# Gram products by pair of heads and ahead of the values, rests at every third column, put-off steps, and quarters of x

## The chip, the cores and the metric

One core of a Trainium2 chip runs the whole layer as one program. Its engines work side by side: TensorE (PE, matrix products), VectorE (DVE), ScalarE (ACT), GpSimd (POOL) and SyncE (SP, which here issues transfers). The metric is device microseconds for one execution. All times below are microseconds.

## The reference

A block of one layer over 256 tokens of width 2048, in float32. The normed input `h` goes through one wide projection, three branches work on the pieces, and their gated results go through a last projection:

```python
h = rms_norm(x, norm_g)
proj = h @ w_in
y_a = merge_heads(moba_attention(...)) * silu(z_a)          # 12 heads of 128
y_b = rwkv7_time_mix(r_b, k_b, v_b, lw, la, ...) * silu(z_b)  # 24 heads of 64
y_c = memory_cross_attention(q_c, mem_n, w_mem_kv) * silu(z_c)
merged = g_a * (y_a @ w_proj_a) + g_b * (y_b @ w_proj_b) + g_c * (y_c @ w_proj_c)
return rms_norm(x + merged @ w_out, final_norm_g)
```

The second branch is a recurrence over the tokens, for each head with a state of 64 x 64:

```python
sa = einsum('bhvk,bhk->bhv', state, a_t)
state = state * w_t + sa * b_t + v_t * k_t      # outer products
y_t = einsum('bhvk,bhk->bhv', state, r_t)
```

## The kernel before

**Main work.** All projections are jobs (class `Job`) that run one after the other in chunks of weights. A chunk of 128 KC x 256 weights is fetched (`raw`, three buffers), split into a high half by ScalarE (L270, a copy to fp32r) and a low half (L273, the rest, by VectorE or in the head by POOL) in `wt` (four buffers), and multiplied. A job in mode "fm" makes the result with features on partitions: for each of four k tiles and two halves of the features one product of 512 columns (L308: the high half with high and low of the input) and one of 256 (L309: the low half). That is eight pairs a chunk. A "wide" job has tokens on partitions and makes twelve products of 512 columns with each half chunk (L306). `prefetch` issues fetches and splits as far ahead as the buffers let it. The input side of the products is hT, the normed and transposed x, split in the same way.

**Side work.** Everything else is written as Python generators, lanes, which are stepped once behind every chunk (`step_lanes`); each yields after how many chunks it wants its next step, and can wait for flags that other lanes set. So the program order on every engine is fixed when the program is written out: a chunk of main products, then a step of each lane that is due, then the next chunk. `force` and `drain` step lanes with no main products between them, until a flag is set or no lane is left. Main products have four banks of PSUM (`pm`), side work has four (`psd`, `ps_side`), which are taken in turn.

**The second branch** runs for six groups of four heads. For a group, `pairs_lane` makes the decays and the tiles AR and BK, transposes two tiles for sums per head (L590) and then the values V and BK (L599 to L601, two sets, one bank each), once the values' job is done, and starts `rw_lane`. That lane computes Gram products of BK and AR (L622, 64 rows of the array each, two chunks of 128 tokens, for each two pairs of heads with two banks each), evacuated on VectorE (L626, L627). It sends 32 x 32 blocks through DRAM into NB and inverts them by a recursion over 31 columns on VectorE (L674, L678), with a rest for one chunk at every fourth column. X goes through DRAM again (XN), and a chain follows on TensorE: L700, L721, L743, L751 to L765 and the transposes of the result (L780), whose bank VectorE reads for the mean and the difference (L790). After a norm (L805 multiplies the values by a sum, L810 adds) comes a last transpose (L817). `attn_a` does the first branch for two heads a group: scores (L838, L840), a softmax (L851 to L861), transposes (L868) and the values' products (L876, L878), whose bank is kept until the gate zsa is there.

**The head.** `x_stats` sums squares of x and keeps TensorE at work with dummy transposes of the identity (L905). Then each quarter of x, 512 columns, is scaled (ScalarE L916 for one half of the tokens, VectorE L917 for the other), transposed (`turned`, L154, eight operations of 128 x 128 a quarter) and evacuated into hT: high halves on ScalarE (L159), low halves on VectorE (L162). `lora_pre` is called ahead of each of the first job's four chunks: it does quarters 0 and 1 ahead of chunk 0, and quarter c + 1 ahead of chunks 1 and 2.

## Time and profile before

| | us |
|---|---|
| three runs | 1478.37, 1479.20 (median), 1479.53 |
| the profiled execution | 1478.29 |
| its span | 1476.5 |
| TensorE busy | 1449.2 (98% of the span) |
| VectorE busy | 946.2 (64%) |
| ScalarE busy | 747.3 (51%) |
| GpSimd busy | 181.8 (12%) |

The span is the time from the first to the last instruction that the profiler records; the execution's own time is measured around it and is 1.8 longer. The busy share of TensorE includes products that are stretched or wait inside a group, so it hides small stalls; the lists of waits and the timelines show them one by one. The granted clock is 0.997 of full speed as a mean over the span.

### The profile page before, as it was taken

To read this page: it belongs to the slowest core of one execution; us is meant where nothing else is said; L and a number is where in the kernel's file an instruction comes from. 1 tells how busy PE (TensorE), PEld (TensorE's weight loads), DVE (VectorE), ACT (ScalarE), POOL (GpSimd) and SP (SyncE) were. 2 spreads that over 40 slices of the span, in tenths; PEclk is the share of its full clock that TensorE was granted. 3 is DMA by queue.
4 is the path that set the end of the run, shared out by engine and by line. 5 is a ranking of instruction groups with operands and counts; after the bars stand their busy time and mean duration, and the time that the engine had idled before them with its cause. 6 is when DMAs were issued, how large, how long until landed. Compare 5 with 4: busy or idle time off the path is not lost.

```text
span 1476.5 us, 22151 instructions
## 1 busy us (share of the span) xinstructions
PE 1449.2 (98%) x8315; PEld 1222.3 (83%) x8315; DVE 946.2 (64%) x1855; ACT 747.3 (51%) x1122; POOL 181.8 (12%) x252
## 2 busy tenths in 40 slices
PE   7999999999999999999999999999999999999997
PEld 6887888888888788788888888888888888888887
DVE  5778697796795786784666555655545545545555
ACT  5546546466456456445666454643443444444443
POOL 4312202212212222211100000000000000000011
PEclk9999999999999999999999999999999999999999
DMA  5665555456465465465575555566556556555753
GB/s 180 192 179 163 159 147 169 143 167 173 133 184 151 134 172 159 135 178 158 162 221 187 172 169 174 167 196 192 187 188 195 188 187 194 188 188 192 262 200 130
DMA packets 207968, 258.88 MB, mean 175 GB/s; under 512 B 28172, under 2 KB 146596, under 8 KB 207220
## 3 DMA queue, kind: packets, MB, share of 16 engines
q1 hardware_dynamic: 201872, 247.11, 54.5%
q10 hardware_dynamic: 4164, 6.71, 1.3%
q0 software_dynamic: 1824, 3.65, 0.8%
q8 instruction: 65, 1.06, 0.3%
q14 instruction: 43, 0.35, 0.1%
HBM read 253.74 MB, written 6.05 MB: 176 GB/s over the span
## 4 chain that ended last, share of the span: by engine, by line
PE 89%; DVE 4%; DMA 2%; ACT 1%; issue 1%; POOL 1%; SPq 0%; ACTq 0%; DVEq 0%
PE pm L306 43%; PE pm L308 24%; PE pm L309 12%; PE psd L622 2%; DVE wt L273 1%; DMA raw<-in_w_in_dram 1%; DVE fs_t L674 1%; PE psd L641 1%; PE psd L1037 1%; PE psd L743 1%; DMA NB<-d 1%; PE psd L154 1%; DMA x_sb<-in_x_dram 1%; ACT wt L270 1%; DVE X L678 1%
## 5 line engine op out<-in xcount | busy, mean ns | idle before, releaser
L273 DVE TENSOR_TENSOR wt<-raw,wt 128x1024 fp32r<-128x1024 f32 (+1 forms) x451 | 559.1, 1242 | 437.4 <-ACT wt L270 433.8
L270 ACT ACTIVATE wt<-raw 128x1024 fp32r<-128x1024 f32 (+1 forms) x452 | 477.2, 1057 | 494.0 <-PE pm L306 256.5
L308 PE MATMUL pm<-hT,wt 128*128 128x512 f32 (+1 forms) x1632 | 587.1, 402 | 0.0
L309 PE MATMUL pm<-hT,wt 128*128 128x256 f32 (+1 forms) x1632 | 458.5, 281 | 3.5 <-DVE wt L273 3.4
L308 PEld LDWEIGHTS pm<-hT,wt 128*128 128x128 f32 (+1 forms) x1632 | 305.7, 187 | 76.3 <-issue 4.2
L306 PE MATMUL pm<-wt,hT 128*128 128x512 f32 x1440 | 335.4, 391 | 0.0
L306 PEld LDWEIGHTS pm<-wt,hT 128*128 128x128 f32 x1440 | 268.6, 188 | 57.6 <-issue 1.7
L309 PEld LDWEIGHTS pm<-hT,wt 128*128 128x128 f32 (+1 forms) x1632 | 307.5, 188 | 6.2 <-DVE wt L273 6.0
L306 PE MATMUL pm<-wt,mg 128*128 128x512 f32 (+1 forms) x384 | 79.3, 367 | 0.0
L306 PEld LDWEIGHTS pm<-wt,mg 128*128 128x128 f32 x384 | 65.7, 189 | 12.5
L1183 POOL MEMSET sso<- 128x16 f32 x1 | 0.1, 117 | 607.0 <-PE pm L306 607.0
L674 DVE TENSOR_TENSOR fs_t<-X,NB 128x30 f32<-128x30 f32 (+13 forms) x354 | 64.9, 223 | 7.5 <-DMA NB<-d 7.1
L306 PE MATMUL pm<-wt,yas 128*128 128x512 f32 x288 | 67.6, 395 | 0.0
L306 PE MATMUL pm<-wt,ybs 128*128 128x512 f32 x288 | 67.6, 395 | 0.0
L323 POOL TENSOR_TENSOR lraw<-lraw,et 128x256 f32<-128x256 f32 (+1 forms) x38 | 45.1, 1207 | 167.2 <-ACT lraw L322 167.2
L306 PEld LDWEIGHTS pm<-wt,ybs 128*128 128x128 f32 x288 | 54.3, 188 | 12.6
L306 PEld LDWEIGHTS pm<-wt,yas 128*128 128x128 f32 x288 | 54.3, 188 | 12.7
L317 ACT ACTIVATE et<-pm 128x256 f32<-128x256 f32 (+1 forms) x112 | 42.6, 382 | 40.3 <-PE pm L309 37.6
L678 DVE TENSOR_TENSOR X<-X,fs_t 128x30 f32<-128x30 f32 (+13 forms) x354 | 56.3, 194 | 0.6
L306 PE MATMUL pm<-wt,mT 128*128 128x512 f32 x192 | 45.8, 395 | 0.0
L308 PE MATMUL pm<-mT,wt 128*128 128x512 f32 x128 | 45.4, 395 | 0.0
L306 PE MATMUL pm<-wt,ycs 128*128 128x512 f32 x192 | 45.3, 395 | 0.0
(299 smaller groups left out, 1324.3 us busy)
## 6 DMA issues: line engine op xcount, KB each, us to landing
raw<-in_w_in_dram SPq DMA_DIRECT2D x320, 512.0 KB, 3.7
raw<-in_w_mem_kv_dram SPq DMA_DIRECT2D x32, 512.0 KB, 3.5
raw<-in_w_out_dram SPq DMA_DIRECT2D x32, 512.0 KB, 4.4
raw<-in_w_proj_a_dram SPq DMA_DIRECT2D x24, 512.0 KB, 4.2
raw<-in_w_proj_b_dram SPq DMA_DIRECT2D x24, 512.0 KB
raw<-in_w_proj_c_dram SPq DMA_DIRECT2D x16, 512.0 KB, 4.4
NB<-d SPq DMA_DIRECT2D x24, 128.0 KB, 3.4
fr<-fd ACTq DMA_DIRECT2D x6, 385.0 KB
```

Of the source, the lines that this page charges most:

```text
L154: pe.transpose(pv[:, a, t], src[:, t, (k + a) * 128:(k + a + 1) * 128], ident)
L270: act.activation(w[:, :, 0], r, AF.Copy)
L273: eng.tensor_tensor(w[:, :, 1], r, w[:, :, 0].bitcast(FT), OP.subtract)
L306: pe.matmul(ps[:, 0:j.n], l, r, start=first and n == 0, stop=last and n == 2)
L308: pe.matmul(ps[0:j.m], hi, both, start=first, stop=last, skip_group_check=True)
L309: pe.matmul(ps[0:j.m, 256:512], lo, top, start=False, stop=last, skip_group_check=True)
L317: act.activation(t, ps[0:j.m, 256:512], AF.Copy)
L323: pool.tensor_tensor(j.dst[f], j.dst[f], t, OP.add)
L622: pe.matmul(pv[h][:, w].rearrange("p x t -> p (x t)"), BK[rows, q, c, w * 128:(w + 1) * 128], AR[rows, q, c].rearrange("p x t -> p (x t)") ...
L641: pe.matmul(pv[:, 2 * q + h], GS[:, c * 4 + 2 * q + h, 2], tok[:, q, c, rows], start=(c == 0), stop=True, skip_group_check=True)
L674: dve.tensor_tensor(t, X[:, k0:8, c:c + 1].to_broadcast([128, m, hi - lo]), NB[:, lo:hi, c].rearrange("p (o n) -> p o n", o=1).to_broadcas ...
L678: dve.tensor_tensor(X[:, k0:8, lo:hi], X[:, k0:8, lo:hi], t, OP.add)
```

## The change

**Gram ahead of the values, a pair of heads a round in chunk 0.** `pairs_lane` transposes the tiles for the sums (L606 after) as soon as BK is made, starts `rw_lane` there, and only then waits for the values. `rw_lane` rests after each pair of heads in chunk 0, not only after the two. New waits for `rkv_free` of the group before guard tiles that are now used earlier.

**The recursion** rests where the column is a multiple of three, below 31: ten times.

**Put-off steps.** A lane can yield a pair (rest, more). When its rest is over, `step_lanes` takes its next step only in a round in which another lane has taken a side bank, or after `more` further rounds. Six places use it, most of them ahead of transposes or products of a full array.

**Quarters of x.** Only quarter 0 is scaled, transposed and evacuated ahead of chunk 0. A new hook of `Job`, `mid`, is called between the two feature halves of a chunk: `lora_mid` transposes and evacuates quarter c + 1 in the middle of chunk c and scales quarter c + 2. Quarter 0 uses a bank for each k tile. Both halves of quarter 1 are scaled on VectorE, the low half of chunk 0's weights goes to POOL, and the dummy transposes come in two halves, the second behind the second half of x.

```diff
+    used = [0]
     def ps_side():
+        used[0] += 1
         return psum.tile([128, 512], FT, name="psd", bufs=4)
...
     def add_lane(gen, rest=0):
-        lanes.append([clock[0] + rest, gen])
+        lanes.append([clock[0] + rest, gen, 0])
...
+    def step(ln):
+        try:
+            d = next(ln[1])
+            d, more = d if isinstance(d, tuple) else (d or 1, 0)
+            ln[0], ln[2] = clock[0] + d, more
+        except StopIteration:
+            lanes.remove(ln)
+
     def step_lanes():
         clock[0] += 1
-        for ln in list(lanes):
-            if ln[0] > clock[0]:
-                continue
-            try:
-                d = next(ln[1])
-                ln[0] = clock[0] + (d or 1)
-            except StopIteration:
-                lanes.remove(ln)
+        n = used[0]
+        due = [ln for ln in lanes if ln[0] <= clock[0]]
+        for ln in due:
+            if not ln[2]:
+                step(ln)
+        for ln in due:
+            if ln[2] and ln[0] <= clock[0]:
+                if used[0] != n or clock[0] >= ln[0] + ln[2]:
+                    ln[2] = 0
+                    step(ln)
...
             products(j, j.ps[f], f, c, w)
+            if f == 0 and j.mid:
+                j.mid(c)
...  (pairs_lane)
         if g:
-            yield from wait(("gram", g - 1))
+            yield from wait(("gram", g - 1), ("rkv_free", g - 1))
...
-        yield 1
-        yield from wait(("V", g))
         yield 1
         for t, o in ((sq, nb), (r, bs)):
             p = ps_side()
...
+        add_lane(rw_lane(g, AR, BK, tok, nb, bs, esc), 2)
+        yield 1
+        yield from wait(("V", g))
+        yield (1, 2)
         v = St.pop(("V", g))
...
-        add_lane(rw_lane(g, AR, BK, tok, nb, bs, esc))
         yield 1
...  (rw_lane)
                     dve.tensor_tensor(GS[:, u, 2:4], pv[h][:, 1], msk, OP.mult)
-            yield 1
+                if c == 0 or q == 1:
+                    yield 1
...
-            if c % 4 == 0:
+            if c % 3 == 0 and c < 31:
                 yield 1
...
         dve.transpose(XT, XN)
+        yield from wait(("rkv_free", g))
         yield 1
...  (x_stats)
         p = ps_side()
-        pe.transpose(p[:, 0:128], x_sb[:, 0, 0:128], ident)
-        for i in range(18):
-            if i == 11:
+        for h in range(2):
+            pe.transpose(p[:, 0:128], x_sb[:, 0, h * D // 2:h * D // 2 + 128], ident)
+            for i in range(10):
+                pe.transpose(p[:, 0:128], ident, ident)
+            if h == 0:
                 turn_params(prow1, "1", 16)
-            pe.transpose(p[:, 0:128], ident, ident)
...
-        issue_split(hold=held)
+        issue_split(pool)
...  (lora_pre)
         if c == 0:
             x_stats()
-            x_quarter(0)
-            x_quarter(1)
-            held.pop()()
-        elif c < 3:
-            x_quarter(c + 1)
-        for f in fins.pop(c):
-            f()
-        if c == 0:
+            x_scale(0)
+            fins = x_turn(0)
+            x_scale(1, dve)
+            for f in fins:
+                f()
             issue_split(pool)
...
+    def lora_mid(c):
+
+        if c < 3:
+            fins = x_turn(c + 1)
+            if c < 2:
+                x_scale(c + 2)
+            for f in fins:
+                f()
```

(In `x_scale` ScalarE scales the first half of the tokens, or VectorE where it is named, and VectorE the second. L322 is the wide product after, L324 and L325 the pair, L286 and L289 the splits, L641 the Gram, L619 to L621 the sets of values.)

TensorE where group 1's values come, before: the result's transposes of group 0 (L780), the sums (L590), the two sets of values, then the Gram.

```order
L306 MATMUL pm<-wt,hT 128x512 x24
L780 MATMUL psd<-ident,YT 128x128 x4
L590 MATMUL psd<-ident,sg 128x128 x4
L590 MATMUL psd<-ident,R 128x128 x4
L599 MATMUL psd<-ident,V 128x128 x2
L600 MATMUL psd<-ident,BK 128x128
L601 MATMUL psd<-ident,BK 128x128
L599 MATMUL psd<-ident,V 128x128 x2
L600 MATMUL psd<-ident,BK 128x128
L601 MATMUL psd<-ident,BK 128x128
L306 MATMUL pm<-wt,hT 128x512 x12
L622 MATMUL psd<-AR,BK 128x256 x8
```

The same place after, from the chain's step L764 of group 0 on:

```order
L322 MATMUL pm<-wt,hT 128x512 x12
L764 MATMUL psd<-W,XF 128x64 x4
L641 MATMUL psd<-AR,BK 128x256 x4
L619 MATMUL psd<-ident,V 128x128 x2
L620 MATMUL psd<-ident,BK 128x128
L621 MATMUL psd<-ident,BK 128x128
L619 MATMUL psd<-ident,V 128x128 x2
L620 MATMUL psd<-ident,BK 128x128
L621 MATMUL psd<-ident,BK 128x128
L322 MATMUL pm<-wt,hT 128x512 x12
```

and one chunk further, from group 0's L784 and L786 to the Gram's second chunk:

```order
L784 MATMUL psd<-GS,tok 64x128
L786 MATMUL psd<-GS,W 64x128
L641 MATMUL psd<-AR,BK 128x256 x4
L322 MATMUL pm<-wt,hT 128x512 x12
L641 MATMUL psd<-AR,BK 128x256 x8
L322 MATMUL pm<-wt,hT 128x512 x12
```

The sums (L606) have moved ahead of these rows. The two sets now follow half of a Gram chunk, whose other half follows L784 and L786, and L801 is no longer beside any of them.

ScalarE in the head, before: splits of weights (L270), scalings of x (L916) and high halves of hT (L159, four a quarter).

```order
L270 ACTIVATE wt<-raw 128x4x192
L916 ACTIVATE x_sb<-x_sb,rs_rn 128x512 x2
L159 ACTIVATE hT<-psd,par_138 128x256 x4
L270 ACTIVATE wt<-raw 128x4x192
L916 ACTIVATE x_sb<-x_sb,rs_rn 128x512
L159 ACTIVATE hT<-psd,par_138 128x256 x4
L270 ACTIVATE wt<-raw 128x4x192
L916 ACTIVATE x_sb<-x_sb,rs_rn 128x512
L159 ACTIVATE hT<-psd,par_138 128x256 x4
L270 ACTIVATE wt<-raw 128x4x192
L159 ACTIVATE hT<-psd,par_138 128x256 x4
```

After, with L286, L938 and L163 for the same:

```order
L286 ACTIVATE wt<-raw 128x4x192
L938 ACTIVATE x_sb<-x_sb,rs_rn 128x512
L163 ACTIVATE hT<-psd,par_137 128x256 x4
L286 ACTIVATE wt<-raw 128x4x192
L938 ACTIVATE x_sb<-x_sb,rs_rn 128x512
L163 ACTIVATE hT<-psd,par_137 128x256 x4
L938 ACTIVATE x_sb<-x_sb,rs_rn 128x512
L163 ACTIVATE hT<-psd,par_137 128x256 x4
L286 ACTIVATE wt<-raw 128x4x192
L163 ACTIVATE hT<-psd,par_137 128x256 x4
L286 ACTIVATE wt<-raw 128x4x192
```

Each of the last two splits of the first job's weights stood ahead of a quarter's four evacuations and now stands behind one quarter's more; on VectorE, L289 stands behind L166 in the same way.

VectorE in group 0's recursion, before: the columns from behind one low half of weights (L273) on. Behind these rows come L857 and the next L273.

```order
L674 TENSOR_TENSOR fs_t<-X,NB 128x40
L674 TENSOR_TENSOR fs_t<-X,NB 128x36
L678 TENSOR_TENSOR X<-X,fs_t 128x4x10
L678 TENSOR_TENSOR X<-X,fs_t 128x4x9
L674 TENSOR_TENSOR fs_t<-X,NB 128x36 x2
L678 TENSOR_TENSOR X<-X,fs_t 128x4x9 x2
L674 TENSOR_TENSOR fs_t<-X,NB 128x36
L674 TENSOR_TENSOR fs_t<-X,NB 128x32
L678 TENSOR_TENSOR X<-X,fs_t 128x4x9
L678 TENSOR_TENSOR X<-X,fs_t 128x4x8
L674 TENSOR_TENSOR fs_t<-X,NB 128x32 x2
L678 TENSOR_TENSOR X<-X,fs_t 128x4x8 x2
```

After, from one low half (L289) to the next:

```order
L289 TENSOR_TENSOR wt<-raw,wt 128x4x256
L694 TENSOR_TENSOR fs_t<-X,NB 128x30 x2
L698 TENSOR_TENSOR X<-X,fs_t 128x3x10 x2
L694 TENSOR_TENSOR fs_t<-X,NB 128x40
L694 TENSOR_TENSOR fs_t<-X,NB 128x36
L698 TENSOR_TENSOR X<-X,fs_t 128x4x10
L698 TENSOR_TENSOR X<-X,fs_t 128x4x9
L694 TENSOR_TENSOR fs_t<-X,NB 128x36 x2
L698 TENSOR_TENSOR X<-X,fs_t 128x4x9 x2
L289 TENSOR_TENSOR wt<-raw,wt 128x4x256
```

Four columns stood between two low halves, now there are three.

## Rows read from the trace of the kernel before

**Rows 1.** Page, chain that ended last: share of the span by engine

```profile
PE 89%; DVE 4%; DMA 2%; ACT 1%; issue 1%; POOL 1%; SPq 0%; ACTq 0%; DVEq 0%
```

**Rows 2.** Waits of TensorE: engine, line, releaser: us in total, times, longest

```profile
PE psd L599 <- DVE Y L790: 3.4, 5, 0.9
PE psd L154 <- ACT x_sb L916: 3.0, 1, 3.0
PE psd L622 <- DVE GS L627: 2.3, 4, 0.6
...
PE psd L700 <- ACT pT L869: 0.4, 1, 0.4
```

**Rows 3.** Timeline, PE: start, us, engine, line, operation, count [idle <-releaser]

```profile
23.09 1.04 PE L154 MATMUL psd<-ident,x_sb 128*128 128x128 f32 x8
...
764.25 0.40 PE L308 MATMUL pm<-hT,wt 128*128 128x512 f32 x1
...
764.61 0.60 PE L154 MATMUL psd<-ident,m_sb 128*128 128x128 f32 x4
764.97 0.48 PE L308 MATMUL pm<-hT,wt 128*128 128x512 f32 x1
```

**Rows 4.** Timeline, PE: L599 in groups 1 and 4

```profile
285.56 0.38 PE L599 MATMUL psd<-ident,V 128*128 128x128 f32 x2
...
286.65 0.41 PE L599 MATMUL psd<-ident,V 128*128 128x128 f32 x2 [0.49 <-DVE Y L790]
...
493.62 0.60 PE L590 MATMUL psd<-ident,R 128*128 128x128 f32 x4
495.15 0.41 PE L599 MATMUL psd<-ident,V 128*128 128x128 f32 x2 [0.93 <-DVE Y L790]
```

**Rows 5.** Timeline, PE: Gram products of groups 0, 1 and 4

```profile
80.42 2.78 PE L622 MATMUL psd<-AR,BK 64*128 64x256 f32 x16
...
290.00 2.00 PE L622 MATMUL psd<-AR,BK 64*128 64x256 f32 x16
...
499.02 1.56 PE L622 MATMUL psd<-AR,BK 64*128 64x256 f32 x10
501.15 1.10 PE L622 MATMUL psd<-AR,BK 64*128 64x256 f32 x6 [0.57 <-DVE GS L627]
```

**Rows 6.** Waits from 104 to 132, all engines

```profile
PEld pm L309 <- DVE wt L273: 3.9, 5, 1.2
```

**Rows 7.** Timeline, DVE and ACT: recursion of group 0

```profile
115.01 0.36 DVE L674 TENSOR_TENSOR fs_t<-X,NB 128x40 f32<-128x40 f32 x2
...
117.06 1.20 DVE L273 TENSOR_TENSOR wt<-raw,wt 128x1024 fp32r<-128x1024 f32 x1
...
118.75 1.28 ACT L206 ACT_TABLE_LOAD   x1
```

**Rows 8.** Timeline, DVE: last steps of the last group

```profile
724.02 1.51 DVE L805 TENSOR_TENSOR Yq<-tok,bs 128x256 f32<-128x256 f32 x1
...
728.87 0.68 DVE L810 TENSOR_TENSOR Y<-Y,Yq 128x512 f32<-128x512 f32 x1
```

**Rows 9.** Windows: us, PE, PEld, DVE, ACT, POOL busy, clock, DMA, GB/s

```profile
13.10:16.50 3.40, 3.25 (x15) 3.26 (x16) 2.29 (x5) 2.79 (x7) 0.00 (x0) 0.50 0.61 181
```

**Rows 10.** Timeline, ACT, DVE and POOL: head

```profile
21.53 0.90 ACT L270 ACTIVATE wt<-raw 128x768 fp32r<-128x768 f32 x1
23.73 1.57 ACT L159 ACTIVATE hT<-psd,par 128x256 fp32r<-128x256 f32 x4 [1.29 <-PE psd L154]
...
16.92 2.12 DVE L917 TENSOR_SCALAR x_sb<-x_sb,rs_rn 128x512 f32<-128x512 f32 x1
...
23.38 0.94 DVE L273 TENSOR_TENSOR wt<-raw,wt 128x768 fp32r<-128x768 f32 x1
24.60 1.66 DVE L162 SCALAR_TENSOR_TENSOR hT<-psd,par,hT 128x256 fp32r<-128x256 f32 x4 [0.28 <-ACT hT L159]
...
16.91 1.85 POOL L273 TENSOR_TENSOR wt<-raw,wt 128x768 fp32r<-128x768 f32 x1 [5.30 <-ACT wt L270]
```

More of the change, by code (lines that the diff above doesn't have):

```diff
@@ L146, in rsqrt_b, with turned @@
         return r
-    def turned(src, g_nm, dst, k):
-        p = ps_side()
-        pv = p.rearrange("p (a t c) -> p a t c", a=2, t=2)
+    def turned(src, g_nm, dst, k, apart=False):
+        banks = [ps_side()]
+        banks.append(ps_side() if apart else banks[0])
+        pv = [two(p)[:, a] for a, p in enumerate(banks)]
         for a in range(2):
             for t in range(2):
-                pe.transpose(pv[:, a, t], src[:, t, (k + a) * 128:(k + a + 1) * 128], ident)
+                pe.transpose(pv[a][:, t * 128:t * 128 + 128], src[:, t, (k + a) * 128:(k + a + 1) * 128], ident)
         def fin():
@@ L158, in fin @@
                 g = pcol(g_nm, k + a)
-                act.activation(dst[:, k + a, 0], two(p)[:, a], AF.Copy, scale=g)
+                act.activation(dst[:, k + a, 0], pv[a], AF.Copy, scale=g)
             for a in range(2):
                 g = pcol(g_nm, k + a)
-                dve.scalar_tensor_tensor(dst[:, k + a, 1], two(p)[:, a], g, dst[:, k + a, 0].bitcast(FT),
+                dve.scalar_tensor_tensor(dst[:, k + a, 1], pv[a], g, dst[:, k + a, 0].bitcast(FT),
                                          op0=OP.mult, op1=OP.subtract)
@@ L240, in tile_hybrid, with __init__ @@
     class Job:
-        def __init__(self, w, c0, n, kt, a, evac, mode="fm", m=128, before=None, pre=None, add=dve):
+        def __init__(self, w, c0, n, kt, a, evac, mode="fm", m=128, before=None, pre=None, mid=None, add=dve):
             self.w, self.c0, self.n, self.kt, self.a = w, c0, n, kt, a
-            self.evac, self.mode, self.m, self.before, self.pre, self.add = evac, mode, m, before, pre, add
+            self.evac, self.mode, self.m, self.before, self.pre, self.mid, self.add = evac, mode, m, before, pre, mid, add
             self.kc = 2 if mode == "wide" else KC
@@ L516, in pairs_lane @@
         pool.dma_start(wa, w_aaa2[0][:, c0:c0 + 256])
-        yield 3
+        yield (3, 2) if g else 3
         p = ps_side()
@@ L834, in attn_a @@
             yield from wait(("soft", g - 1))
+        yield (1, 2)
         q, k = St[("qa", g)], St[("ka", g)]
@@ L885, in tile_hybrid @@
     norm_r = []
-    fins = {}
     consts = []
-    held = []
     def x_stats():
@@ L909, in x_stats, with x_scale, x_turn @@
         issue_dma(nc.scalar)
-        issue_split(hold=held)
+        issue_split(pool)
         norm_r.append(rsqrt_b(v, s, 2, "n"))
-    def x_quarter(q):
+    def x_scale(q, first=act):
         r, cs = norm_r[0], slice(512 * q, 512 * q + 512)
-        act.activation(x_sb[:, 0, cs], x_sb[:, 0, cs], AF.Copy, scale=r[:, 0:1])
+        if first is act:
+            act.activation(x_sb[:, 0, cs], x_sb[:, 0, cs], AF.Copy, scale=r[:, 0:1])
+        else:
+            dve.tensor_scalar(x_sb[:, 0, cs], x_sb[:, 0, cs], r[:, 0:1], None, op0=OP.mult)
         dve.tensor_scalar(x_sb[:, 1, cs], x_sb[:, 1, cs], r[:, 1:2], None, op0=OP.mult)
-        fins[q] = [turned(x_sb, "g", hT, 4 * q + 2 * a) for a in range(2)]
+    def x_turn(q):
+        return [turned(x_sb, "g", hT, 4 * q + 2 * a, apart=(q == 0)) for a in range(2)]
     def lora_pre(c):
```

6 lines of the change are left out of this document (3 added, 3 removed).

## The prediction

> **What bounds the kernel now.** I read the chain that ended last first, to see which engine the end hangs on: TensorE holds 89% of it, VectorE 4% [rows 1]. So a change gains only where TensorE stands still or is slowed down, and loses where it makes TensorE wait. The list of TensorE's waits came next [rows 2]. It names four places the change touches: the transposes of L599 that wait for L790 (3.4 us in five waits), the Gram products L622 that wait for L627 (2.3 in four), the main products L309 that wait for the low halves of weights, L273 ([rows 6] has their weight loads in one stretch), and the first transposes of x, L154 (3.0, once). L700 waits 0.4 for attention's L869. Last came the timelines around those rows, for a wait that is listed is shorter than what the path loses by it. A pair of main products is 0.36 long (L308 at 764.25 to the next operation at 764.61, [rows 3]), a feature-major chunk of eight pairs therefore 2.8 to 2.9.
>
> **Merging excursions and putting steps off: 0.** Four transposes between main products push the next L308 back by 0.36, from 764.61 to 764.97, and the eight of 23.09 are listed with 1.04 against 0.60 for four, so 0.11 each and nothing for going there and back [rows 3]. Two steps of full-array work that now share one gap therefore save nothing. What hides a put-off step is the row of main products in between; it delays its own lane by at most two chunks. Bounds: -0.5 to +0.5, the rows for 0.
>
> **A: the second set of L599, -3.8.** Before, L780, two times L590 and two sets of L599 follow each other. There are four banks, so the second set needs L780's, which VectorE's L790 reads only after both reductions. In group 1 the first set starts at 285.56, the second should 0.44 later (four transposes, as from L780 to L590) and starts at 286.65: 0.65 lost. In group 4 the first set should start at 494.06, 0.44 after the last L590, and starts at 495.15: 1.09 lost, [rows 4]. Groups 1 to 3 are like the one and 4 and 5 like the other: 3 x 0.65 + 2 x 1.09 = 4.1. Now the reductions stand a chunk or more ahead, L780 stands elsewhere, and what precedes the sets is one pair of Gram products. What is late next is the second set in groups 4 and 5, where attention's last product holds one of the four banks and three turn: it follows the evacuation of a Gram bank. I charge 0.3 for both together. Bounds: -4.1, if nothing waits, and -2.0, if the new neighbour's evacuation takes half of it back.
>
> **B: Gram products, -3.2.** One chunk of the Gram is 16 products in 2.00 where nothing disturbs them (290.00). In group 4 it goes from 499.02 to 501.15 plus 1.10, or 3.23: 1.23 lost, with three banks left. In group 0 it is 2.78: 0.78 lost [rows 5]. Groups 4 and 5 have two such chunks each. The change takes chunk 0 of every group apart by pair of heads, with at least one other step between, so two banks are enough: 0.78 + 2 x 1.23 = 3.2 goes. Chunk 1 is still two pairs in one go and keeps its two waits. Bounds: -3.2, and -1.6, if the second pair of heads comes so soon behind other side work that half is kept.
>
> **C: a further piece of narrow work in each group, +0.6.** Gram products use 64 rows of the array. In one piece 16 of them take 2.00; in two pieces 10 and 6 take 1.56 and 1.10 [rows 5], which is 0.66 more in listed time, most of it each piece's end, which the next main product overlaps. Chunk 0 was one piece, now it is two, in six groups. The row bounds it by 0 and 6 x 0.3 = 1.8; I take 0.1 a group, near the lower end, because one of the two pieces now stands directly beside another narrow step (L764 or L784 and L786 in the order), where the array is narrow already.
>
> **D: the recursion rests at every third column, -2.2.** In the stretch from 104 to 132, group 0's recursion, weight loads wait 3.9 for L273 [rows 6]. Four columns on VectorE take from 115.01 to 117.06, or 2.05, and the low half of a chunk 1.20: 3.25 for each chunk of 2.8 to 2.9 [rows 7]. With three columns it is 1.54 + 1.20 = 2.74, just under. So the stock of split chunks no longer shrinks in the recursion itself. Not all goes: ScalarE's table load of 1.28 at 118.75 [rows 7] and the softmax around it also hold splits up, and they stay. I keep 1.7 of the 3.9. Bounds: -3.9, and 0, if ScalarE alone was the cause. The recursion is three chunks longer (ten rests for seven); what is queued behind it on SyncE are the four writes of X and the four reads of XN, and behind these the chain L700 to L780. In the order each step of that chain still has a chunk of main products ahead of it, and the next group's Gram stays where it was, so I cost this at nothing; if that cover goes it is the rival on the other side below.
>
> **E and the drain: -0.4 and +0.8.** L700's wait [rows 2] goes, since attention's transposes no longer stand just ahead of it. At the end of the last group the later chain means that its last transposes (L817 before) fall into the stretch where all lanes are emptied with no main products between. They then wait for VectorE's L805 and L810, 1.51 and 0.68 at 724.02 and 728.87 [rows 8]. Bounds 0 and 2.2, their sum; I take 0.8, nearer the last addition alone.
>
> **F: the head, +3.7.** Before, sixteen transposes of x come first, then eight ahead of chunks 1 and 2 each. Now eight come first, and the next quarter's eight stand in the middle of a chunk. In this stretch the granted clock is 0.50 (13.10 to 16.50) and 15 operations take 3.25, 0.22 each [rows 9], so eight fewer give up to 1.7 ahead of the first main product. But chunk 0's low half moves to POOL, where such a half took 1.85 at 16.91, against 0.94 on VectorE at 23.38, and VectorE's scaling beside it took 2.12 (16.92) [rows 10]. That eats the lead; I take 0 for the start, bounds -1.2 and +1.
> The Trainium skill (SBUF — State Buffer, Who interferes with whom) has it that VectorE and GpSimd share a pair of ports and that the loser blocks for the other's whole instruction. The rows of 16.91 and 16.92 agree with it; without the lock the start would be some 1.2 earlier, and the rest of this sum unchanged.
> The cost comes in chunks 2 and 3. In the order, ScalarE's high half (L286) and VectorE's low half (L289) of these chunks now stand behind the evacuations (L163 and L166) of the quarter that is transposed in the middle of the chunk before. Count from the first of those transposes, with rows of [rows 10]: ScalarE starts 0.64 later (23.09 to 23.73, [rows 3, 10]), takes 1.57 and then 0.90 for the high half, ending at 3.1; VectorE starts its four at 1.51 (24.60), ends at 3.17, and the low half takes 0.94, ending at 4.1. TensorE needs 0.85 for eight transposes and 1.43 for four pairs, and wants the low half at about 2.5. So 1.6 of waiting in each of two chunks: 3.2. Before, the half stood ahead of the evacuation (21.53 before 23.73) and was ready. Chunk 4's splits queue behind these: +0.5. Bounds for the head as a whole: -1, if the lead at the start covers it, and +6.
>
> **The sum.** -3.8 - 3.2 + 0.6 - 2.2 - 0.4 + 0.8 + 3.7 = -4.5. The profiled execution took 1478.3 (a span of 1476.5 and 1.8 around it), so it would take 1473.8. The median of the three runs, 1479.2, lies 0.9 above it and gives 1474.7; I say 1474.3.
>
> **Rivals.** *The head and ScalarE give it all back (no change).* F at its upper bound, +6, and D at 0: -3.8 - 3.2 + 0.6 - 0.4 + 0.8 + 6 = 0.0, about 1478 to 1479; with only one of them at its bound, 1476 to 1477. For it: the queue orders of ScalarE and VectorE in the head are facts of the program, and every operation in them has a row. Against it: POOL takes over a half that was on VectorE, and PE arrives later at chunk 4, where it waits already.
> *The longer recursion pushes its chain against the next due time (slower).* Three chunks later per group, the chain L700 to L780 would meet a job that demands its results, and steps would then follow each other with no main products between. Each group has some five such steps, each waiting for an evacuation like the 0.68 of L810 or the 1.09 of [rows 4], say 0.9: 5 x 0.9 x 5 groups = 22 at most. It decides from about a third of that: +8 on top of -4.5 gives 1482.7. For it: the drain shows one such place. Against it: the order has main products between those steps in groups 1 to 4.
> *The head runs ahead (a larger gain).* The dummy transposes are now in two halves, the second after the second half of x. Before, TensorE stood idle for 3.0 ahead of the first transposes [rows 2] and the granted clock was at its lower level, 1.2 GHz, right after [rows 9]. If it stays at 2.4 GHz, eight transposes save 0.9 and the start moves ahead of POOL's half; with D at its lower bound the sum is -4.5 - 0.9 - 1.7 - 2 = -9, or 1470. The Trainium skill (TensorE: Matmul & The Clock Gate, HAM oscillation) ties the lower level to idle time of the engine; these two rows agree with it. Against it: a gap of two us or more remains while ScalarE and VectorE work out the norm.
>
> **How the numbers follow.** The forecast (1472 to 1476.2) has a chance of 0.47, the larger gain 0.13, no change 0.29, slower 0.11. A measurement of this kernel tells about 0.2%, 3 us, from no change, so below 1476.2 counts as faster: 0.60; between that and 1482.2 same: 0.29; above: 0.11. The range leaves out about a tenth on each side: from 1468.5, beyond the larger gain's centre, to 1481.5, which takes in nearly all of the case of no change. Its own range for the forecast is 1472 to 1476.
>
> **What would show it.** In the profile after: no wait of the second L619 set above 0.3 (A); chunk 0 of the Gram in two pieces of about 1 us each, chunk 1 of groups 4 and 5 still at 3.2 (B, C); fewer than 2 us of weight loads waiting for L289 between 104 and 132 (D); main products waiting for L289 by about 1.6 at the starts of chunks 2 and 3, with L166 just ahead of L289 on VectorE (F). I am wrong if the head shows no such waits, if the recursion's stretch still waits 3 us or more, or if the chain L721 to L801 waits in every group.

## The result and the profile after

The changed kernel is slower: 1489.78 us (median of six, 1485.75 to 1490.03) against 1479.37 (median of six, 1476.89 to 1480.07), a ratio of 1.0068 with a 95% interval of 1.0055 to 1.0081. The forecast was 1474.3 (1472 to 1476.2). The profiled execution took 1489.73 with a span of 1488.0, 11.5 more than before.

Both kernels run the same 6368 main products in the same order, so a start of the same product in both traces tells how late the changed kernel is by then. Worked out from the two traces:

| up to main product (start before) | what lies in the stretch | late by, us | of it in the stretch |
|---|---|---|---|
| 128 (43.7) | head | +4.85 | +4.85 |
| 960 (232.8) | group 0's recursion and chain, Gram of group 1 and its recursion | +0.63 | -4.2 |
| 1408 (337.4) | group 1's chain and tail, Gram of group 2 and its recursion | +2.81 | +2.2 |
| 1824 (441.3) | group 2's chain, Gram of group 3 | +2.43 | -0.4 |
| 2280 (548.3) | group 3's chain, group 4's recursion | +4.77 | +2.3 |
| 2736 (658.1) | group 4's chain, group 5's recursion | +6.34 | +1.6 |
| 3024 (733.4) | group 5's chain | +5.47 | -0.9 |
| 3072 (742.0) | all lanes emptied | +11.56 | +6.1 |

Behind that nothing changes any more. Group 0's stretch gave back nearly all that the head had lost; the later groups lost again, and over half of the difference comes in the last stretch of phase one. Side work that moves past the end of a stretch is counted in the next one: the +6.34 at product 2736 is +0.93 at 2784, since group 5's chain, which before starts at 2764, comes later after the change. The list of TensorE's waits in the changed kernel (us in total, times, longest; compare [rows 2]):

```profile
PE pm L325 <- DVE wt L289: 8.8, 8, 2.2
...
PE psd L838 <- DVE Y L831: 5.7, 3, 4.0
PE psd L641 <- DVE GS L646: 1.1, 2, 0.6
PE psd L619 <- DVE GS L646: 0.8, 2, 0.4
PE pm L324 <- ACT wt L286: 0.6, 1, 0.6
```

L619's wait for the mean's bank is gone (3.4 in [rows 2]), L641's is half of the 2.3 before, and there is a new one, L838 on L831, of 5.7 in three waits, one of them 4.0. The low halves of weights, L289, cost 8.8 in eight waits.

**The head.** Timeline of the changed kernel's TensorE, ScalarE and VectorE from the transposes in the middle of chunk 1 (22.43) on; compare [rows 10]:

```profile
25.42 0.48 PE L324 MATMUL pm<-hT,wt 128*96 128x512 f32 x1 [0.57 <-ACT wt L286]
26.51 0.36 PE L325 MATMUL pm<-hT,wt 128*96 128x256 f32 x1 [0.62 <-DVE wt L289]
...
23.06 1.57 ACT L163 ACTIVATE hT<-psd,par 128x256 fp32r<-128x256 f32 x4 [1.54 <-PE psd L158]
24.50 0.86 ACT L286 ACTIVATE wt<-raw 128x768 fp32r<-128x768 f32 x1
...
23.93 1.66 DVE L166 SCALAR_TENSOR_TENSOR hT<-psd,par,hT 128x256 fp32r<-128x256 f32 x4 [1.66 <-ACT hT L163]
25.51 0.95 DVE L289 TENSOR_TENSOR wt<-raw,wt 128x768 fp32r<-128x768 f32 x1
```

The high half L286 starts behind the evacuations of ScalarE, the low half L289 behind those of VectorE, and the first pair of chunk 2 waits for each in turn: 0.57 and 0.62 of listed idle time, 1.6 in all against the usual pitch. Chunk 3 waits for its low half alone, 0.9. At chunk 4 the wait is 1.08, where the kernel before already had 0.6 (its L309 at 31.20), so 0.5 is new. The first main product came 0.9 earlier, at 15.64, but chunk 1 starts 0.77 later than before: the four pairs from 15.64 on are 0.65 apart instead of 0.35, and the eight transposes behind them take 1.18 instead of 0.79. The trace's first record of the granted clock is 1.00 from 19.12 on (in the kernel before from 9.69 on, then 0.50 from 13.10 to 16.52), and only from there is the pace the usual one.

**Bank waits.** Timeline of TensorE at the values and the Gram of groups 2 and 4; compare [rows 4, 5] (the rows at 285 and 290 there, which the prediction puts in group 1, are group 2's, and groups 1 to 3 are alike):

```profile
283.63 1.13 PE L641 MATMUL psd<-AR,BK 64*128 64x256 f32 x8
284.70 0.44 PE L619 MATMUL psd<-ident,V 128*128 128x128 f32 x2
...
285.19 0.38 PE L619 MATMUL psd<-ident,V 128*128 128x128 f32 x2
...
495.04 0.44 PE L619 MATMUL psd<-ident,V 128*128 128x128 f32 x2
...
496.11 0.41 PE L619 MATMUL psd<-ident,V 128*128 128x128 f32 x2 [0.41 <-DVE GS L646]
...
505.37 1.56 PE L641 MATMUL psd<-AR,BK 64*128 64x256 f32 x10
507.50 1.10 PE L641 MATMUL psd<-AR,BK 64*128 64x256 f32 x6 [0.57 <-DVE GS L646]
```

In group 2 the two sets of values follow each other in 0.49, with no wait. In group 4 the second set now waits 0.41 for the evacuation of a Gram bank (L646), and chunk 1 of the Gram has the same stall as before.

**Group 4's recursion.** VectorE, then TensorE, then windows of the stretch (us; PE, PEld, DVE, ACT, POOL busy; clock; DMA share; GB/s):

```profile
540.95 1.23 DVE L289 TENSOR_TENSOR wt<-raw,wt 128x1024 fp32r<-128x1024 f32 x1 [2.63 <-ACT wt L286]
542.09 0.87 DVE L841 SCALAR_TENSOR_TENSOR yb<-psd,par,zsb 128x256 f32<-128x256 f32 x2
...
544.36 0.68 DVE L867 SCALAR_TENSOR_TENSOR as<-psd,bias 128x512 f32<-128x512 f32 x1
544.96 0.41 DVE L868 SCALAR_TENSOR_TENSOR as<-psd,bias 128x256 f32<-128x256 f32 x1
545.29 1.00 DVE L873 TENSOR_REDUCE amx<-as 128x2 f32<-128x512 f32 x2
546.21 1.21 DVE L289 TENSOR_TENSOR wt<-raw,wt 128x1024 fp32r<-128x1024 f32 x1
```

```profile
544.89 0.39 PE L324 MATMUL pm<-hT,wt 128*128 128x512 f32 x1
547.48 0.39 PE L325 MATMUL pm<-hT,wt 128*128 128x256 f32 x1 [2.20 <-DVE wt L289]
```

```profile
545.00:548.00 3.00, 0.80 (x5) 0.48 (x4) 3.00 (x6) 2.81 (x6) 1.15 (x2) 1.00 0.08 28
...
549.00:550.00 1.00, 1.00 (x5) 0.90 (x4) 1.00 (x10) 1.00 (x6) 0.84 (x3) 0.50 0.93 272
```

Between two low halves VectorE has the previous group's last step (L841), three columns and all of attention's scores (L867 to L873), 5.3 us from 540.95 to 546.21, where a chunk of main products takes 2.8. TensorE stands for 2.20, and then runs at the lower level of its clock, 0.50, for 3.4 us (548.19 to 551.60). Before, L820 ran at 527.3 and the scores (L845 to L851) from 537.4, ten us apart, and TensorE's wait there was below 0.2.

**Group 1's tail and the last stretch.** TensorE (326.44 is the last transpose of group 1) and VectorE of the changed kernel; compare [rows 8]:

```profile
326.44 0.66 PE L838 MATMUL psd<-ident,Y 128*128 128x128 f32 x4 [1.43 <-DVE Y L831]
...
741.61 0.28 PE L325 MATMUL pm<-hT,wt 128*128 128x256 f32 x1
745.88 0.84 PE L838 MATMUL psd<-ident,Y 128*128 128x128 f32 x4 [4.00 <-DVE Y L831]
746.38 0.77 PE L324 MATMUL pm<-hT,wt 128*128 128x512 f32 x1
```

```profile
739.36 1.85 DVE L826 TENSOR_TENSOR Yq<-tok,bs 128x256 f32<-128x256 f32 x2
741.13 0.68 DVE L491 TENSOR_TENSOR zsb<-zsb,et 128x512 f32<-128x512 f32 x1
741.73 2.88 DVE L289 TENSOR_TENSOR wt<-raw,wt 128x1024 fp32r<-128x1024 f32 x2
744.53 1.21 DVE L831 TENSOR_TENSOR Y<-Y,Yq 128x512 f32<-128x512 f32 x1
```

At 745.88 L838 follows the last main product at once and waits for L826, L491, two low halves (L289) and L831 in VectorE's queue: 4.00, and the next product takes 0.77 instead of some 0.48. The same queue stood in the trace before, where main products covered it:

```profile
723.69 1.85 DVE L805 TENSOR_TENSOR Yq<-tok,bs 128x256 f32<-128x256 f32 x2
725.46 0.68 DVE L881 TENSOR_TENSOR ya<-psd,zsa 128x512 f32<-128x512 f32 x1
726.06 2.89 DVE L273 TENSOR_TENSOR wt<-raw,wt 128x1024 fp32r<-128x1024 f32 x2
```

The row at 724.02 in [rows 8] is the second of the two L805; from the first to the end of L810 it is 5.9 us.

### The profile page after: what moved, and what is told of

It is laid out like the page before. It is cut to its first block, busy times and chain, and to the rows that moved or that the text cites. A ratio compares the mean times of both kernels' runs of the same rounds, so it can differ in the third digit from the quotient of the medians.

```text
span 1488.0 us, 22149 instructions
## 1 busy us (share of the span) xinstructions
PE 1453.6 (98%) x8318; PEld 1225.6 (82%) x8318; DVE 946.7 (64%) x1855; ACT 748.4 (50%) x1121; POOL 180.0 (12%) x253
## 3 DMA queue, kind: packets, MB, share of 16 engines
q0 software_dynamic: 1824, 3.65, 0.8%
## 4 chain that ended last, share of the span: by engine, by line
PE 84%; DVE 6%; DMA 5%; ACT 2%; issue 1%; SPq 1%; DVEq 0%; ACTq 0%
PE pm L322 42%; PE pm L324 21%; PE pm L325 10%; DMA raw<-in_w_in_dram 3%; DVE wt L289 2%; PE psd L641 2%; DVE fs_t L694 1%; DMA NB<-d 1%; ACT wt L286 1%; PE psd L1069 1%; PE psd L764 1%; PE psd L661 1%; DVE X L698 1%; PE psd L784 0%; PE psd L746 0%
## 5 line engine op out<-in xcount | busy, mean ns | idle before, releaser
L289 DVE TENSOR_TENSOR wt<-raw,wt 128x1024 fp32r<-128x1024 f32 (+1 forms) x450 | 558.9, 1244 | 422.1 <-ACT wt L286 419.7
L286 ACT ACTIVATE wt<-raw 128x1024 fp32r<-128x1024 f32 (+1 forms) x452 | 476.6, 1056 | 494.6 <-PE pm L322 267.7
L324 PE MATMUL pm<-hT,wt 128*128 128x512 f32 (+1 forms) x1632 | 590.9, 404 | 1.1 <-ACT wt L286 0.6
L325 PE MATMUL pm<-hT,wt 128*128 128x256 f32 (+1 forms) x1632 | 461.2, 283 | 8.9 <-DVE wt L289 8.8
L324 PEld LDWEIGHTS pm<-hT,wt 128*128 128x128 f32 (+1 forms) x1632 | 308.1, 189 | 77.0 <-issue 2.5
L322 PE MATMUL pm<-wt,hT 128*128 128x512 f32 x1440 | 335.2, 391 | 0.0
L325 PEld LDWEIGHTS pm<-hT,wt 128*128 128x128 f32 (+1 forms) x1632 | 310.2, 190 | 12.5 <-DVE wt L289 12.3
L322 PEld LDWEIGHTS pm<-wt,hT 128*128 128x128 f32 x1440 | 268.6, 188 | 57.3 <-issue 1.3
L322 PE MATMUL pm<-wt,mg 128*128 128x512 f32 (+1 forms) x384 | 79.3, 367 | 0.0
L322 PEld LDWEIGHTS pm<-wt,mg 128*128 128x128 f32 x384 | 65.7, 189 | 12.5
L694 DVE TENSOR_TENSOR fs_t<-X,NB 128x30 f32<-128x30 f32 (+13 forms) x354 | 67.8, 231 | 10.4 <-DMA NB<-d 10.2
L322 PE MATMUL pm<-wt,yas 128*128 128x512 f32 x288 | 67.6, 395 | 0.0
L322 PE MATMUL pm<-wt,ybs 128*128 128x512 f32 x288 | 67.6, 395 | 0.0
L322 PEld LDWEIGHTS pm<-wt,yas 128*128 128x128 f32 x288 | 54.3, 188 | 12.6
L322 PEld LDWEIGHTS pm<-wt,ybs 128*128 128x128 f32 x288 | 54.3, 188 | 12.6
L322 PE MATMUL pm<-wt,mT 128*128 128x512 f32 x192 | 45.8, 395 | 0.0
L324 PE MATMUL pm<-mT,wt 128*128 128x512 f32 x128 | 45.4, 395 | 0.0
L322 PE MATMUL pm<-wt,ycs 128*128 128x512 f32 x192 | 45.3, 395 | 0.0
```

Source lines behind the costliest of these rows:

```text
L286: act.activation(w[:, :, 0], r, AF.Copy)
L289: eng.tensor_tensor(w[:, :, 1], r, w[:, :, 0].bitcast(FT), OP.subtract)
L322: pe.matmul(ps[:, 0:j.n], l, r, start=first and n == 0, stop=last and n == 2)
L324: pe.matmul(ps[0:j.m], hi, both, start=first, stop=last, skip_group_check=True)
L325: pe.matmul(ps[0:j.m, 256:512], lo, top, start=False, stop=last, skip_group_check=True)
L694: dve.tensor_tensor(t, X[:, k0:8, c:c + 1].to_broadcast([128, m, hi - lo]), NB[:, lo:hi, c].rearrange("p (o n) -> p o n", o=1).to_broadcas ...
```

## The experiments

Each kernel was timed beside the kernel before on the same chip; the ratio is to that. "Alone" means as an edit of the kernel before.

| run | what it has | median, us | ratio (95%) |
|---|---|---|---|
| p1 | new head alone | 1484.73 | 1.0032 (1.0020 to 1.0044) |
| p2 | rests alone | 1483.30 | 1.0025 (1.0014 to 1.0035) |
| p3 | Gram alone | 1480.24 | 1.0004 (0.9995 to 1.0013) |
| p4 | put-off steps without those of the Gram | 1482.65 | 1.0015 (1.0006 to 1.0023) |
| p5 | Gram and rests | 1483.61 | 1.0028 (1.0017 to 1.0038) |
| p6 | p5, last group rests at every fourth | 1479.88 | 1.0000 (0.9991 to 1.0010) |
| p7 | changed, old head | 1484.31 | 1.0031 (1.0020 to 1.0042) |
| p8 | p1, splits ahead of the evacuations | 1481.67 | 1.0011 (1.0002 to 1.0020) |
| p9 | p3, L801 one chunk later | 1483.47 | 1.0021 (1.0012 to 1.0029) |
| p10 | p9, rests of three in group 0 | 1479.82 | 0.9999 (0.9991 to 1.0008) |
| p11 | changed, rests at every fourth column | 1483.72 | 1.0020 (1.0010 to 1.0030) |
| p12 | two pieces, where they gain | 1476.37 | 0.9976 (0.9968 to 0.9985) |

The kernel before had medians of 1479.83 to 1480.17 beside them. My theory from the trace of the changed kernel: the head costs what its own rows show, and the rests, which move the tail of each group three chunks on, into the next recursion and in the last group into the stretch without main products, cost the rest. The rival: the put-off steps do, by moving attention's scores.

**p1, the head alone.** The kernel before with `x_scale`, `x_turn`, `lora_mid`, the hook `mid` and the dummies of the changed kernel.

```diff
-jobs = [Job(w_in2, LW, ..., pre=lora_pre, add=pool)]
+jobs = [Job(w_in2, LW, ..., pre=lora_pre, mid=lora_mid, add=pool)]
```

> The kernel before with the head alone changed (quarters of x, hook mid, POOL for chunk 0, dummies in two halves). Theory (the head costs by itself what the first 41 us of the changed kernel show, and nothing later gives it back): main products 4.7 to 4.9 us late from the first job's end on, total 4 to 5.5 us over the kernel before, about 1484. Rival (the two reserves absorb it, since the stalls of before at 30 and 58 us go): 1 to 3 us over.

It was 4.75 over. Nothing later absorbs it: in the trace, which is of p1's fastest execution (1482.00), main products are 4.0 late behind the head and 3.7 at the end. TensorE there reaches its usual pace at 17.0 instead of 19.1.

**p2, the rests alone.**

```diff
-            if c % 4 == 0:
+            if c % 3 == 0 and c < 31:
```

> The kernel before with the recursion resting at every third column, nothing else. Theory (the rests move the tail of every group three chunks later, into the next recursion and attention, and the last one into the stretch that empties all lanes): waits of the last transposes L817 of about 4 us at the end of phase one and 1 to 2 in the middle groups, one or two stalls of 2 us on low halves in groups 4 and 5, less about 2 for the recursion of group 0: 4 to 9 us over before. Rival (the put-off steps make those stalls, by moving attention's scores into the recursion): only the last wait of 4 remains, less 2: 0 to 3 over.

It was 3.3 over, between the two: just above the rival's range and a little under the theory's. Three of its waits (us in total, times, longest):

```profile
PE pm L309 <- DVE wt L273: 6.3, 12, 0.8
...
PE psd L817 <- DVE Y L810: 4.0, 1, 4.0
...
PE psd L622 <- DVE GS L627: 2.3, 4, 0.6
```

The wait at the end of phase one is the 4.0 of the changed kernel, with no put-off step in this one; no other wait of L817 is listed, where the theory had some in the middle groups. The recursions of groups 4 and 5 stall by 2.2 and 2.3 against the usual pitch, in three waits each (540 to 549 and 649 to 658); no granted clock below 1.00 follows these. What I had not expected is on the gain side: no wait of L599 on L790 is listed any more. The rests move the result's transposes away from the values by themselves, so term A belongs to them. The Gram's own waits (L622) are as before.

**p3, the Gram alone.** The Gram part of the diff, with `yield 1` where the change puts steps off.

```diff
+        add_lane(rw_lane(g, AR, BK, tok, nb, bs, esc), 2)
+        yield 1
         yield from wait(("V", g))
...
+                if c == 0 or q == 1:
+                    yield 1
```

> The kernel before with the Gram ahead of the values and a pair of heads a round in chunk 0, with no put-off steps, rests at every fourth column and the old head. Theory (terms A to C of the prediction hold): 4.5 to 6.5 us under before, about 1473.5. Rival (bank waits only change places): within 1.5 us of before.

The rival holds, 0.3 over. The list of waits shows where the stall went:

```profile
PE psd L641 <- DVE Y L811: 2.8, 5, 0.9
```

The result's transposes (L801), the two sets and the Gram's first pair now meet in one round, five banks for four, and the Gram waits for L811 instead of the values.

**p4, the put-off steps alone.** `step_lanes` and four of the tuples of the change (it has five, not six; the fifth belongs to the Gram part), without its Gram, rests and head.

> The kernel before with the put-off steps alone. Theory (they only move steps between neighbouring chunks, at no cost): within 2 us of before. Rival (they push attention's scores and softmax three chunks on, into the recursion): stalls of about 2 us on low halves in groups 4 and 5, 3 to 6 us over before.

2.7 over, between the two. The recursions of groups 4 and 5 stall by 1.2 and 1.1 (551 and 660), where the kernel before has less than 0.2. In the profiled execution it was 1.2 ahead of the kernel before at main product 2640; between 2688 and 2784 it lost 6.1, around one wait:

```profile
PE psd L718 <- DMA XN<-d: 1.8, 2, 1.5
```

```profile
666.00:667.00 1.00, 1.00 (x5) 1.00 (x6) 0.00 (x0) 0.00 (x0) 0.00 (x0) 0.50 0.96 367
```

In group 5 the chain's first step stands one chunk earlier, at main product 2752 instead of 2764, ahead of the transfer that brings XN. The granted clock is 0.50 behind it, from 664.8 to 671.7. But this execution is the slowest of p4's eleven (1484.41), and p8, whose program is there that of the kernel before, loses 4.2 at the same place in its slowest execution, with a wait of 0.5 for XN at product 2764 and the clock at 0.50 from 671.1 to 677.9. So what the earlier step costs p4 as a rule is not shown.

The four parts add up: 4.75 + 3.3 + 0.3 + 2.7 = 11.0, against 10.4 for the change as a whole. That is partly chance, for their effects depend on each other: below, the put-off steps cost 0.7 on top of Gram and rests (p7 over p5), and the rests 6.1 on top of everything else (the changed kernel over p11).

**p5, Gram and rests together.** The edits of p2 and p3.

> Gram ahead of the values and rests at every third column together, old head, no put-off steps. Alone the one gave nothing, since its first Gram products came right behind the transposes L801 and waited for their bank, and the other 3.7 us more. Theory (the two need each other: the rests move L801 three chunks on, away from the Gram): the bank waits of L641 on L811 go, 4.5 to 7 us under the rests alone, 1477 to 1479; the wait of 4 us at the end of phase one stays. Rival (the Gram order saves nothing wherever the transposes stand): 1483 to 1484.

The rival again: 1483.61, as the rests alone. The rests had already taken A's gain, so the Gram had only B's and C's to add, and these are small: main product by main product against p2, the stretch from the sums to chunk 1 of the Gram gives 0.85 + 1.02 - 2.03 = -0.2 in group 4, the same in group 5, and a loss of 0.85 + 0.37 - 0.86 = 0.35 in each of groups 1 to 3, where the Gram had no stall to lose. Its waits on low halves:

```profile
PE pm L325 <- DVE wt L289: 5.0, 10, 0.8
```

**p6, the last group's rests as before.**

```diff
-            if c % 3 == 0 and c < 31:
+            if (c % 3 == 0 and c < 31) if g < NG - 1 else c % 4 == 0:
```

> As the run with Gram and rests together, but the last group rests at every fourth column as before. Theory (nearly all that the rests cost is the last group's transposes in the stretch where all lanes are emptied: a wait of 4 us, and the lower granted clock behind it): that wait goes, 6 to 8 us under the run with Gram and rests, 1470 to 1473. Rival (the rests cost in every group): at most 2 us under it.

3.7 under p5, between the two and half of what I gave it. The wait of 4.0 at the end is gone, but group 5's recursion, four columns a round again and with group 4's later tail in it, has stalls of 1.7, 0.9 and 1.0 between 647 and 656. So p6 only comes back to the kernel before: in its trace it is 2.9 ahead at product 2640 and has lost 5.9 by 2784.

**p7, the changed kernel with the old head.**

> The changed kernel with the old head: Gram, rests and put-off steps. Theory (the put-off steps move attention's scores into the longer recursion, which makes the stalls of 2 us at 545 and 655 of the changed kernel): 5 to 8 us over the run with Gram and rests, about 1485, and 4 to 5.5 under the changed kernel. Rival (those stalls come from Gram and rests): within 2 us of the run with Gram and rests, which then has them too.

0.7 over p5: the rival holds, though 5.5 under the changed kernel is as the theory had it. Its waits on low halves:

```profile
PE pm L325 <- DVE wt L289: 7.6, 7, 2.2
```

The recursions of groups 4 and 5 stall by 2.8 and 2.3 here and by 2.4 and 2.2 in p5, only nearly all in one piece instead of three. With the rests the put-off steps add little to those stalls; without them they make about half as much (p4, p11). What they do change is the clock: it falls to 0.50 behind the single pieces of 2.22 and 2.10, and does not behind the three shorter ones of p5.

**p8, splits ahead of the evacuations.** p1 with one more line, so that the splits of chunks 2 and 3 come first:

```diff
             fins = x_turn(c + 1)
+            if c:
+                issue_split()
```

> The kernel before with the new head, but the splits of chunks 2 and 3 issued ahead of the evacuations in the middle of chunks 1 and 2. Theory (the head's cost is splits that queue behind evacuations on ScalarE and VectorE): the waits at the starts of chunks 2 and 3 go, 2.5 to 4 us under the run with the head alone, 1480.5 to 1482. Rival (the transposes in the middle of chunks, or the clock, cost it): within 1 us of 1484.7.

3.1 under p1 by the medians, as expected. ScalarE's rows (compare the changed kernel's 24.50):

```profile
20.79 0.86 ACT L271 ACTIVATE wt<-raw 128x768 fp32r<-128x768 f32 x1
...
23.07 1.57 ACT L160 ACTIVATE hT<-psd,par 128x256 fp32r<-128x256 f32 x4 [0.80 <-PE psd L155]
```

The high half L271 now stands ahead of L160, and no main product of chunks 2 and 3 waits. The median is still 1.5 over the kernel before. In the trace the head ends 2.2 late, against 4.0 in p1: 0.8 by the start of chunk 1, at the lower pace, 0.8 for the last eight transposes, which now come in chunk 2, and 0.5 at chunk 4, whose wait of 1.08 stays. (The profiled execution is p8's slowest, 1486.61; 4.2 of that is the stretch in group 5 that p4's paragraph names, far behind the head.)

**p9, the result's transposes one chunk later.** p3, and in groups 0 to 4:

```diff
-        yield 1
+        yield 2 if g < NG - 1 else 1
         Y = rw.tile([128, 8, 64], FT, name="Y")
```

> Gram ahead of the values with a pair of heads a round, old head, rests at every fourth column, no put-off steps (the run that came out within 0.3 of before), and the transposes of the result (L801) one chunk later in groups 0 to 4. Theory (there the stall on the bank of L811 only moved from the values to the Gram, 2.8 in five waits; it goes where the result's transposes share no round with the values): those five waits go, 2.5 to 4.5 us under that run, 1476 to 1477.5. Rival (the wait moves again, to the Gram's second pair): within 1 us of 1480.

Neither: 3.2 over p3 by the medians, though the two profiled executions took the same 1481.6. The five bank waits did go, but a tail that is later by one chunk already met group 2's recursion. TensorE and VectorE there:

```profile
318.91 0.63 PE L838 MATMUL psd<-ident,Y 128*128 128x128 f32 x4 [1.76 <-DVE fs_t L694]
```

```profile
316.93 1.23 DVE L289 TENSOR_TENSOR wt<-raw,wt 128x1024 fp32r<-128x1024 f32 x1 [1.71 <-ACT wt L286]
318.07 0.69 DVE L831 TENSOR_TENSOR Y<-Y,Yq 128x512 f32<-128x512 f32 x1
```

L838 stands for 1.76, and 1.9 more are lost to low halves from 333 to 341.

**p10, rests of three in group 0 as well.**

> As the run before it, with rests at every third column in group 0 alone. Theory (in group 0 the rests give back 1 to 2 us and its later tail meets no stall): 0.5 to 2 us under the run before it, 1475 to 1476.5. Rival (group 0's tail, later, meets the recursion of group 1 as it does in groups 4 and 5): 0 to 2 us over it.

3.7 under p9, more than expected: 1479.82. The recursion of group 0 has one stall of 0.8 instead of 2.7 in three, and L838 waits 0.8 instead of 1.76 at 321; a stall of 1.5 at 231 is new. The two spans of the profiled executions differ by 1.3 only; why the medians of p9 and p10 are further apart was not settled.

**p11, the changed kernel with rests at every fourth column.**

> The changed kernel with rests at every fourth column: head, Gram and put-off steps stay. Theory (the rests of three make the wait of 4 us at the end of phase one, the waits of L838 at 325 and 644 and most of the stalls at 320, 545 and 655; against that they keep the result's transposes away from the Gram and shorten group 0's recursion): 4 to 7 us under the changed kernel, 1483 to 1486, with bank waits on L811 of 2.8 to 3.4 back, and stalls of about 1 in groups 4 and 5. Rival (the stalls come from put-off steps): 1 us or less under it.

6.1 under the changed kernel, 1483.72, as the theory had it: no wait of L838 is listed, groups 4 and 5 stall by 1.3 and 1.0, and L619 waits for L811 again, if by less than forecast:

```profile
PE psd L619 <- DVE Y L811: 1.9, 5, 0.7
PE psd L721 <- DMA XN<-d: 1.4, 2, 1.2
```

The second row is the place of p4 again: group 5's chain starts at product 2752 and waits for XN, the granted clock is 0.50 from 667.2 to 670.6, and this execution, the median one, loses 4.1 to the kernel before between 2736 and 2784. That and the head, 4.5, are more than all that p11 is over.

**p12, two pieces where they gain.** Rests of three in group 0 alone; the Gram ahead of the values, a pair of heads a round, in groups 4 and 5 alone; old head, no put-off steps.

```diff
+            if (c % 3 == 0 and c < 31) if g == 0 else c % 4 == 0:
+                if q == 1 or (c == 0 and g >= 4):
+                    yield 1
+        early = g >= 4      # rw_lane starts ahead of the wait for V
```

> The kernel before with two pieces of the change only where the traces show them to gain: rests at every third column in group 0, and the Gram ahead of the values, a pair of heads a round, in groups 4 and 5. Theory (each part gains where it does not move a group's tail into a recursion that already fills VectorE): about 1 us in group 0's recursion, 0.65 on the bank of group 1, 0.7 in each of groups 4 and 5, 1.5 to 3.5 us under before. Rival (VectorE's timetable has no room for any shift): within 1 us of before or over it.

3.5 under the kernel before (2.2 to 4.7 by the interval), at the end of the theory's range: the fastest of all. In the trace group 0's recursion and what lies beside it give 2.5, groups 4 and 5 0.7 each, and the head and group 1's stretch lose 0.5 and 1.1. Its waits:

```profile
PE pm L325 <- DVE wt L289: 2.9, 5, 0.9
...
PE psd L648 <- DVE Y L818: 1.9, 2, 0.9
PE psd L624 <- DVE Y L818: 1.0, 2, 0.5
```

It keeps bank waits on L818, in groups 2 to 5, and two stalls of 0.8 and 1.0 at 227 to 231, where group 0's later tail meets group 1's recursion.

## Why the prediction was wrong

**A, -3.8: right, by another cause.** The waits went (in the whole side work between main products the changed kernel needs 5.6 less than before, leaving out L838, L746 and the head; A, B, C and E together were forecast at -6.8). But the rests do it, as p2 shows, and not the Gram order, which alone moves the wait on to the Gram (p3). "L780 stands elsewhere" was true of the whole change, but it is owed to the rests, which the prediction did not say.

**B, -3.2, and C, +0.6: B too large, C too small.** Group 0 did gain the 0.8 in the changed kernel. In groups 4 and 5 the stall of chunk 0 went, but the second set of values now waits 0.41 for a Gram bank, and the further piece of narrow products costs more than C's 0.1. Net of that each gains 0.2 (p5 against p2) to 0.4 (the changed kernel against p2), not 1.2, and groups 1 to 3 lose 0.3 to 0.35 each.

**D, -2.2 for group 0's recursion: right.** Weight loads waited 1.8 instead of 3.9 [rows 6] there (2.5 with the rests alone, p2):

```profile
PEld pm L325 <- DVE wt L289: 1.8, 3, 1.0
```

**F, +3.7: right in its mechanism at chunks 2 and 3, and near in size (4.85) partly by luck.** New waits at chunks 2, 3 and 4 are 1.6, 0.9 and 0.5, where F had 1.6, 1.6 and 0.5; p8 shows that the place in the queue is the cause at chunks 2 and 3. The start was not the 0 that F took: the lead of 0.9 was gone within chunk 0, whose first four pairs ran 0.65 apart instead of 0.35, and the last eight transposes cost 0.8 in chunk 2. The rival of a larger gain counted on the higher level from the dummies on; the pace of the rows was the lower one up to 19.1.

**The step that failed** is in D and in the drain: "In the order each step of that chain still has a chunk of main products ahead of it ... so I cost this at nothing", and +0.8 for the last transposes. I had looked for main products on TensorE between the steps. What the steps need is room on VectorE, and the tail of a group (L826, L831, L841: 1.85 at 739.36, 0.68 at 325.70, 0.87 at 542.09) moved by three chunks into rounds that the next recursion and attention's scores already filled. It costs 2.2 in each of groups 4 and 5 (p2), in the changed kernel a wait of 1.4 for L838 at 325 and one of 1.4 for a low half at 322, and at the end 4.0 instead of 0.8, since two low halves of weights stand in VectorE's queue between the addition and what it needs. I had bounded that wait by the product and the addition alone, 2.2, taking one of the two products L805 for both, and left out what else is queued on VectorE ahead of the addition, though the trace before showed it. By the changed kernel's trace the terms that came as gains were A, B, C and E with -5.6 and D with -2, and F added 4.85: together some -2.8. The span is 11.5 longer, so some 14 us lie in what I had put at 0 and 0.8. The rows show roughly where: 5.7 for L838, 5.65 for the low halves at 322, 547 and 657, and about 4 for the lower clock behind three of these waits.

"Put off: 0" failed too, with 2.7 alone and 0.7 on top of Gram and rests. The stalls of 1.2 and 1.1 in p4's groups 4 and 5 are shown; that the rest of its cost is a step that lost its chunk of cover for a transfer is what the traces of p4 and p11 suggest, and no run here moves that step alone.

The rival that the longer recursion pushes its chain had the right part of the program but the wrong mechanism, a job that forces results; the list of waits has 0.3 for the whole chain L721 to L801, and where all lanes are emptied only L838 waits. Its chance, 0.11, was too low, because a tail that is moved lands somewhere, and I did not list what stands there.

**The lower clock was not priced.** After idle times of 2.20, 2.07 and 4.00 us (544.89, 655.10, 741.61) pairs are 0.64 apart instead of 0.35 for some five pairs each, about 1.4 us each time. The one of the six executions that took 1485.75, 4 us less than the median, agrees with that: its mean granted clock is 0.998, where the others have 0.994 or 0.995. It has no trace.

## What to carry to other kernels

Where program order is fixed and TensorE is nearly always busy, price a later step by what its engine already has in the rounds where it lands: write that engine's list for those rounds, with durations, and hold it against the length of a chunk. A wait that goes may be owed to another part of the change than the one meant for it, so try the parts alone: here two of four pieces, used only in the groups where the traces showed them to gain, gave 3.5 us, and the whole cost 10.4. Parts that add up to the whole have not been shown to be independent: try them on top of each other as well.

## What the runs showed of the hardware

In the middle of the kernel the granted clock fell to 0.50, 1.2 GHz, wherever TensorE stood idle for 2.07 us or more, for 3.4 us in the changed kernel and 6.8 behind the 4.00 of p2. Below that the length of the idle time does not sort the cases: after 1.43 (at 326 in the changed kernel), 1.53 (650 in p6), 1.64 (123 in p11) and 1.76 (319 in p9) it stayed at 1.00, but it fell after 1.50 (664 in p4), 1.19 (665 in p11) and, in p8, at 671.1, behind a wait of 0.54 that ended at 669.0 and as one of 0.64 began. These three falls lie around the first products of group 5's chain, 32 x 32 each (L718, L721, L703); whether that matters was not tried. In the head of the changed kernel transposes were 0.21 and pairs 0.65 apart, the pace of the lower level, while the windows there list 1.00: the trace has no record of the granted clock ahead of 19.12, and a stretch without a record is listed as 1.00. So the pace of the rows has to be read beside that column. The scaling of x on VectorE took 2.04 and 1.90 beside POOL's low halves (12.76 and 16.68) and 0.47 alone, as in [rows 10].
